# A two-layer decoder trunk on one core: the tile of right-hand operands begins 64 bytes later

## The chip, the cores and the metric

The kernel runs on one core of a Trainium2 chip, as one program in one launch. The metric is the device time in microseconds (us). A core has a matrix engine (TensorE, PE in the profile; PEld is its loading of weights), a vector engine (DVE), a scalar engine (ACT), GpSimd (POOL) and SyncE (SP), which here only issues transfers. They share an on-chip memory (SBUF) of 128 partitions, in which a tile takes the same bytes of every partition.

## The reference

The trunk has 512 tokens of 1024 features and two layers. Everything is float32.

```
h = x
for i in range(DEPTH):
    h = h + 0.5 * swiglu(rms_norm(h, norm_ffn_a[i]), ffn_a_wg[i], ffn_a_wu[i], ffn_a_wd[i])
    hn = rms_norm(h, norm_mix[i])
    mix = even_mixer(hn, ...) if i % 2 == 0 else odd_mixer(hn, ...)
    h = h + mix
    h = h + 0.5 * swiglu(rms_norm(h, norm_ffn_b[i]), ffn_b_wg[i], ffn_b_wu[i], ffn_b_wd[i])
    gate = jax.nn.sigmoid(rms_norm(h, norm_ple[i]) @ ple_gate[i])
    h = h + gate * (p[i] @ ple_proj[i])
return rms_norm(h, final_norm)

def swiglu(h, wg, wu, wd):
    return (jax.nn.silu(h @ wg) * (h @ wu)) @ wd
```

The even mixer runs a sparse attention over the 128 best keys beside a differential attention; the odd one a mixture of three dilated windows. The hidden width of a feed-forward block is 2816.

## The kernel before, in words

The residual stream lies transposed in eight tiles `h0` to `h7`, 128 features by 512 tokens each. Every float32 operand of a large product is split into a high part and a rest, both in the type float32r, and a product is three matmuls: high by high, high by rest, rest by high. In a matmul one operand is stationary (128 columns, loaded as weights ahead of it) and the other moves through, 256 to 512 columns here.

The tile `xr` (line 57) holds right-hand operands: 128 partitions by 2 parts (high, rest) by 7168 float32r. It is allocated once, behind `h7`, and is followed in the code by `hid` (hidden activations, line 63), `hl` (split weights, five slots, line 66) and `fr` (raw weights and scratch, line 69). Tiles of the pool are laid one behind the other in the order of the code; `xr` begins on a multiple of 128 bytes, as do `hid`, `hl` and `fr`. Three things use `xr`:

- In the feed-forward blocks it is seen as `xr[:, part, op, i, :]` (line 58): seven combinations `op` of the halves of the normed input, four blocks `i`, 256 columns each, so 1024 bytes in a row. `right` (line 363) builds them: ACT copies the high part (line 372), DVE takes the rest (line 373). `rest` (line 383) fills two of the seven late. `pair` (line 451) runs a Strassen-like scheme of seven products over them into the accumulators X, Y and Z; its matmul is line 463, with `hl` stationary and `xr` moving. `down` (line 502) multiplies the hidden activations from `hid` with the next weights, by way of `mm3` (lines 306 to 309); it does not touch `xr`. The steps of `pair` and `down` alternate in an order that `plan_ffn` writes out.
- In the mixers the columns from 3072 on of both parts hold the normed input as `xh` and `xl` (lines 59 and 60, written by lines 352 and 353). There it is the stationary operand of `project` (line 608), and `hl` moves. The weight pieces of the first projection hold two rows of 456 columns each, 1824 bytes; those of the others hold rows of 256 or 384 columns.
- The columns ahead of these hold the values of the attention in the mixers (`vts`, line 61, lines 747 and 748), stationary in `attend`; and some operands of the gated embeddings (line 361) and of an output projection (line 755).

Weights are loaded by DMA into `fr`, split by ACT (line 173) and DVE (line 175) into a slot of `hl`, and used from there; a sum of weights that the scheme needs is made by DVE at line 164. A framework orders the instructions of each engine and places the semaphores.

Of the kernel before, what the change touches and what calls it, by code (L numbers as in the profile page):

```python
# [12 lines left out]
F32R = mybir.dt.float32r  # L13
# [5 lines left out]
P = 128  # L19
# [19 lines left out]
def trunk(ctx, tc, a, stop=None):  # L39
# [3 lines left out]
    const = ctx.enter_context(tc.tile_pool(name="const", bufs=1))  # L43
# [10 lines left out]

    hT = [const.tile([P, NT], F32, tag=f"h{c}", name=f"h{c}") for c in range(KD)]

    xrt = const.tile([P, 2, 7168], F32R, tag="xr", name="xr")
    xr = xrt.rearrange("p s (o i n) -> p s o i n", o=7, i=4)
    xh = [xrt[:, 0, 3072 + c * NT : 3072 + (c + 1) * NT] for c in range(KD)]
    xl = [xrt[:, 1, 3072 + c * NT : 3072 + (c + 1) * NT] for c in range(KD)]  # L60
# [1057 lines left out]
```

## Time and profile before

| | us |
|---|---|
| median of 3 runs | 2203.91 |
| lowest, highest | 2203.74, 2205.78 |
| the profiled execution | 2205.18 |
| its span, first to last instruction | 2203.4 |
| PE busy in the span | 2081.2 |
| DVE, ACT, POOL busy | 1698.5, 1068.8, 281.2 |

The profile shows one execution. Busy time counts an instance from its start to its end and overlapping ones once; a matmul's end lies some way behind the start of the next, so what one costs in a stream is read from the distance of the starts in the timeline, not from its duration. The mean granted clock of TensorE is 0.966 of its full 2.4 GHz over the span. In the views below "X<-xr,hl" means that the instruction writes X and reads xr and hl, and 128x256 is partitions by elements.

### The profile page before, as it was taken

To read this page: it belongs to the slowest core of one execution; us is meant where nothing else is said; L and a number is where in the kernel's file an instruction comes from. 1 tells how busy PE (TensorE), PEld (TensorE's weight loads), DVE (VectorE), ACT (ScalarE), POOL (GpSimd) and SP (SyncE) were. 2 spreads that over 40 slices of the span, in tenths; PEclk is the share of its full clock that TensorE was granted. 3 is DMA by queue.
4 is the path that set the end of the run, shared out by engine and by line. 5 is a ranking of instruction groups with operands and counts; after the bars stand their busy time and mean duration, and the time that the engine had idled before them with its cause. 6 is when DMAs were issued, how large, how long until landed. Compare 5 with 4: busy or idle time off the path is not lost.

```text
span 2203.4 us, 34325 instructions
## 1 busy us (share of the span) xinstructions
PE 2081.2 (94%) x13283; PEld 1906.9 (87%) x13283; DVE 1698.5 (77%) x2682; ACT 1068.8 (49%) x1722; POOL 281.2 (13%) x249
## 2 busy tenths in 40 slices
PE   4999999998787899999999999999999879999998
PEld 3999998988676899999789999989989769999986
DVE  7888776688987887786688877767656688877775
ACT  4544444355555454443455444445656545444443
POOL 2000000433411000000320000014324110000011
PEclk6999999999899899999999999999999979999999
DMA  4333233321211233333233333222212214333331
GB/s 128 106 104 100 86 95 104 79 60 47 61 39 39 77 96 106 111 102 94 84 95 101 101 101 115 87 80 77 68 48 71 77 39 121 94 93 107 108 111 41
DMA packets 302051, 190.06 MB, mean 86 GB/s; under 512 B 14208, under 2 KB 292800, under 8 KB 301888
## 3 DMA queue, kind: packets, MB, share of 16 engines
q1 hardware_dynamic: 298592, 184.36, 28.5%
q10 hardware_dynamic: 2912, 2.46, 0.4%
q8 instruction: 104, 1.70, 0.3%
q0 software_dynamic: 384, 1.05, 0.2%
q14 instruction: 59, 0.48, 0.1%
HBM read 185.73 MB, written 2.10 MB: 85 GB/s over the span
## 4 chain that ended last, share of the span: by engine, by line
PE 85%; DVE 11%; issue 1%; ACT 1%; DMA 1%; POOL 0%; SPq 0%; DVEq 0%; POOLq 0%; ACTq 0%
PE X L463 23%; PE Y L463 11%; PE down L308 7%; PE down L307 7%; PE down L309 7%; PE Z L463 6%; PE proj L307 3%; PE proj L308 3%; PE proj L309 3%; DVE fr L164 1%; DVE xr L373 1%; PE outp L308 1%; PE outp L307 1%; PE pt L716 1%; PE outp L309 1%
## 5 line engine op out<-in xcount | busy, mean ns | idle before, releaser
L173 ACT ACTIVATE hl<-fr 128x1024 fp32r<-128x1024 f32 (+5 forms) x620 | 521.8, 860 | 681.8 <-PE X L463 301.7
L175 DVE TENSOR_TENSOR hl<-fr,hl 128x1024 fp32r<-128x1024 f32 (+2 forms) x485 | 548.0, 1137 | 164.7 <-ACT hl L173 159.2
L463 PE MATMUL X<-xr,hl 128*128 128x256 f32 x4224 | 551.4, 286 | 27.8 <-DVE xr L373 25.0
L463 PEld LDWEIGHTS X<-xr,hl 128*128 128x128 f32 x4224 | 534.0, 194 | 39.5 <-DVE xr L373 29.0
L463 PE MATMUL Y<-xr,hl 128*128 128x256 f32 x2112 | 279.6, 287 | 19.9 <-ACT xr L372 11.2
L463 PEld LDWEIGHTS Y<-xr,hl 128*128 128x128 f32 x2112 | 265.2, 194 | 26.7 <-ACT xr L372 12.5
L308 PE MATMUL down<-hid,hl 128*128 128x512 f32 x704 | 274.8, 390 | 0.0
L307 PE MATMUL down<-hid,hl 128*128 128x512 f32 x704 | 274.7, 390 | 0.0
L309 PE MATMUL down<-hid,hl 128*128 128x512 f32 x704 | 274.3, 390 | 0.0
L164 DVE TENSOR_TENSOR fr<-fr 128x1024 f32<-128x1024 f32 x176 | 218.8, 1244 | 23.1 <-DMA fr<-in_ffn_b_wu_dram 11.1
L175 POOL TENSOR_TENSOR hl<-fr,hl 128x512 fp32r<-128x512 f32 (+3 forms) x135 | 155.6, 1170 | 270.2 <-ACT hl L173 220.5
L307 PE MATMUL proj<-hl,xr 128*128 128x384 f32 (+2 forms) x512 | 170.1, 335 | 5.6 <-DVE fr L632 4.3
L308 PE MATMUL proj<-hl,xr 128*128 128x384 f32 (+2 forms) x512 | 170.0, 333 | 0.0
L309 PE MATMUL proj<-hl,xr 128*128 128x384 f32 (+2 forms) x512 | 169.9, 334 | 0.0
L309 PEld LDWEIGHTS down<-hid,hl 128*128 128x128 f32 x704 | 132.3, 188 | 26.8
L307 PEld LDWEIGHTS down<-hid,hl 128*128 128x128 f32 x704 | 132.4, 188 | 26.0
L308 PEld LDWEIGHTS down<-hid,hl 128*128 128x128 f32 x704 | 132.5, 188 | 24.8
L463 PE MATMUL Z<-xr,hl 128*128 128x256 f32 x1056 | 149.6, 284 | 1.1 <-ACT hl L173 0.9
L463 PEld LDWEIGHTS Z<-xr,hl 128*128 128x128 f32 x1056 | 137.1, 193 | 1.7 <-ACT hl L173 1.2
L640 POOL TENSOR_TENSOR fr<-fr 128x512 f32<-128x512 f32 (+1 forms) x72 | 90.9, 1268 | 222.4 <-DVE fr L632 106.6
L512 DVE TENSOR_TENSOR fr<-down,fr 128x512 f32<-128x512 f32 x128 | 87.9, 687 | 22.7 <-PE down L309 21.8
L307 PEld LDWEIGHTS proj<-hl,xr 128*128 128x128 f32 x512 | 98.0, 191 | 7.6 <-DVE fr L632 4.5
(211 smaller groups left out, 2925.5 us busy)
## 6 DMA issues: line engine op xcount, KB each, us to landing
fr<-in_ffn_a_wg_dram SPq DMA_DIRECT2D x88, 256.0 KB, 3.1
fr<-in_ffn_a_wu_dram SPq DMA_DIRECT2D x88, 256.0 KB, 3.5
fr<-in_ffn_b_wg_dram SPq DMA_DIRECT2D x88, 256.0 KB, 3.1
fr<-in_ffn_b_wu_dram SPq DMA_DIRECT2D x88, 256.0 KB, 3.4
fr<-in_ffn_a_wd_dram SPq DMA_DIRECT2D x48, 384.0 KB, 3.8
fr<-in_ffn_b_wd_dram SPq DMA_DIRECT2D x48, 384.0 KB, 3.7
fr<-in_odd_w_in_dram SPq DMA_DIRECT2D x96, 128.0 KB, 2.4
fr<-in_even_w_in_dram SPq DMA_DIRECT2D x56, 128.0 KB, 2.7
```

The costliest lines, as they stand in the source:

```text
L164: nc.vector.tensor_tensor(src, *(sums[x] if isinstance(x, int) else x.ap() for x in (a, b)), op=ALU.add)
L173: nc.scalar.activation(hi[:, s:e], src[:, s:e], AF.Copy)
L175: eng.tensor_tensor(lo[:, s:e], src[:, s:e], hi[:, s:e].bitcast(F32), op=ALU.subtract)
L307: nc.tensor.matmul(ps, lh, rh, start=first, stop=False)
L308: nc.tensor.matmul(ps, lh, rl, start=False, stop=False)
L309: nc.tensor.matmul(ps, ll, rh, start=False, stop=last)
L373: nc.vector.tensor_tensor(lw, s, h.bitcast(F32), op=ALU.subtract)
L463: nc.tensor.matmul(o, w[lw][:, i, us], xr[:, r, op, i, :], start=start and u == 0 and i == 0 and n == 0, stop=i == 3 and n == 2, skip_grou ...
L512: nc.vector.tensor_tensor(t, ps, state["R"], op=ALU.mult)
L640: nc.gpsimd.tensor_tensor(dst, rv, tv, op=ALU.add)
L716: nc.tensor.transpose(ps[:, off : off + P], es[b][:, c * P : (c + 1) * P], ident)
```

## The change

The tile `xr` becomes 14368 float32r long, 32 more than before, and the kernel uses the 14336 from the 16th on, so that everything in it lies 16 elements, 64 bytes, further on in each partition. The view is then shaped as before. All other tiles stay where they were, up to the 32 elements by which the tile is longer. No other line changes.

```
-    xrt = const.tile([P, 2, 7168], F32R, tag="xr", name="xr")
+    xrt = const.tile([P, 14368], F32R, tag="xr", name="xr")[:, 16:14352].rearrange(
+        "p (s n) -> p s n", s=2)
     xr = xrt.rearrange("p s (o i n) -> p s o i n", o=7, i=4)
```

## Rows read from the trace of the kernel before

**Rows 1.** The page's head: busy time of each engine over the whole span

```profile
span 2203.4 us, 34325 instructions
...
PE 2081.2 (94%) x13283; PEld 1906.9 (87%) x13283; DVE 1698.5 (77%) x2682; ACT 1068.8 (49%) x1722; POOL 281.2 (13%) x249
```

**Rows 2.** The chain that ended last: shares by engine, then by line

```profile
PE 85%; DVE 11%; issue 1%; ACT 1%; DMA 1%; POOL 0%; SPq 0%; DVEq 0%; POOLq 0%; ACTq 0%
PE X L463 23%; PE Y L463 11%; PE down L308 7%; PE down L307 7%; PE down L309 7%; PE Z L463 6%; PE proj L307 3%; PE proj L308 3%; PE proj L309 3%; DVE fr L164 1%; DVE xr L373 1%; PE outp L308 1%; PE outp L307 1%; PE pt L716 1%; PE outp L309 1%
```

**Rows 3.** Busy us (x instructions) by stretch; PEclk is the granted clock

```profile
core 0: us, PE busy (x) PEld busy (x) DVE busy (x) ACT busy (x) POOL busy (x), PEclk, DMA share, GB/s
...
400.00:600.00 200.00, 177.34 (x1072) 162.37 (x1070) 170.63 (x503) 97.90 (x239) 86.95 (x78) 0.93 0.21 57
600.00:800.00 200.00, 172.99 (x1035) 150.60 (x1036) 164.95 (x305) 106.24 (x197) 17.65 (x13) 0.90 0.20 57
800.00:1000.00 200.00, 200.00 (x1426) 189.06 (x1425) 157.74 (x164) 89.20 (x103) 0.00 (x0) 1.00 0.35 103
...
1200.00:1400.00 200.00, 200.00 (x1421) 188.88 (x1420) 161.62 (x169) 90.09 (x105) 0.00 (x0) 1.00 0.33 98
...
1800.00:2000.00 200.00, 200.00 (x1482) 191.63 (x1481) 160.65 (x163) 95.12 (x109) 0.00 (x0) 1.00 0.35 102
```

**Rows 4.** PE groups by line and form: count, busy us, mean ns, idle before

```profile
L463 PE MATMUL X<-xr,hl 128*128 128x256 f32 x4224 | 551.4, 286 | 27.8 <-DVE xr L373 25.0 <-ACT xr L372 2.7
L463 PE MATMUL Y<-xr,hl 128*128 128x256 f32 x2112 | 279.6, 287 | 19.9 <-ACT xr L372 11.2 <-DVE xr L373 8.7
...
L463 PE MATMUL Z<-xr,hl 128*128 128x256 f32 x1056 | 149.6, 284 | 1.1 <-ACT hl L173 0.9 <-DVE hl L175 0.2
...
L307 PE MATMUL proj<-hl,xr 128*128 128x384 f32 x384 | 130.6, 342 | 1.3 <-DVE xr L748 1.3
```

**Rows 5.** Timeline of PE, 62 to 80 us: start us, us, line, count

```profile
66.80 5.92 PE L463 MATMUL X<-xr,hl 128*128 128x256 f32 x48
72.56 3.04 PE L463 MATMUL Y<-xr,hl 128*128 128x256 f32 x24
75.44 0.40 PE L463 MATMUL Z<-xr,hl 128*128 128x256 f32 x2
```

**Rows 6.** Timeline of PE in the first projections, 378 to 450 us

```profile
403.73 0.37 PE L307 MATMUL proj<-hl,xr 128*128 128x456 f32 x1
403.94 0.36 PE L308 MATMUL proj<-hl,xr 128*128 128x456 f32 x1
...
412.00 0.37 PE L309 MATMUL proj<-hl,xr 128*128 128x456 f32 x1
412.22 0.28 PE L307 MATMUL proj<-hl,xr 128*128 128x256 f32 x1
412.33 0.28 PE L308 MATMUL proj<-hl,xr 128*128 128x256 f32 x1
412.45 0.28 PE L309 MATMUL proj<-hl,xr 128*128 128x256 f32 x1
...
412.93 0.28 PE L307 MATMUL proj<-hl,xr 128*128 128x256 f32 x1
```

**Rows 7.** Timeline of PE, 1310 to 1322 us: a down step behind line 463

```profile
1314.41 3.04 PE L463 MATMUL X<-xr,hl 128*128 128x256 f32 x24
1317.29 0.40 PE L308 MATMUL down<-hid,hl 128*128 128x512 f32 x1
...
1318.45 0.39 PE L307 MATMUL down<-hid,hl 128*128 128x512 f32 x1
...
1321.85 0.39 PE L307 MATMUL down<-hid,hl 128*128 128x512 f32 x1
```

**Rows 8.** Groups of DVE, then of ACT, by form; columns as in rows 4

```profile
L175 DVE TENSOR_TENSOR hl<-fr,hl 128x1024 fp32r<-128x1024 f32 x324 | 395.2, 1228 | 114.2 <-ACT hl L173 110.7 <-DMA fr<-in_x_dram 2.4 <-PE rbc L340 0.7
...
L373 DVE TENSOR_TENSOR xr<-fr,xr 128x1024 fp32r<-128x1024 f32 x16 | 23.0, 1440 | 6.5 <-ACT xr L372 6.3
...
L373 DVE TENSOR_TENSOR xr<-fr,xr 128x768 fp32r<-128x768 f32 x12 | 13.6, 1129 | 0.0
...
L173 ACT ACTIVATE hl<-fr 128x1024 fp32r<-128x1024 f32 x324 | 339.5, 1058 | 453.6 <-PE X L463 241.4 <-DVE fr L164 73.5 <-PE Y L463 48.0
...
L372 ACT ACTIVATE xr<-fr 128x1024 fp32r<-128x1024 f32 x16 | 16.9, 1054 | 16.9 <-DVE fr L379 16.7
```

**Rows 9.** Waits of PE, longest in total first: us, times, longest us

```profile
PE X L463 <- DVE xr L373: 25.0, 12, 4.5
PE Y L463 <- ACT xr L372: 11.2, 4, 4.6
PE Y L463 <- DVE xr L373: 8.7, 8, 2.1
```

## The prediction

> **What bounds the kernel now.** I read the page's head first: TensorE (PE) is busy for 94% of the span, VectorE (DVE) for 77%, ScalarE (ACT) for 49% [rows 1]. A busy PE can still wait inside, so the chain that ended last comes next: 85% of it is PE, 11% DVE, and line 463, the Strassen-like products of the feed-forward blocks, holds 23 + 11 + 6 = 40% of it [rows 2]. Then the stretches: in 800 to 1000, 1200 to 1400 and 1800 to 2000 us PE has no idle time at all, at a granted clock of 1.00 (its 2.4 GHz level), while DVE is busy for 158 to 162 us of 200. In the mixers (400 to 800 us) PE is idle for 23 to 27 us of 200 and its clock averages 0.90 to 0.93 [rows 3]. So a nanosecond on a matmul of line 463 is a nanosecond on the end; on a matmul of the mixers it is worth a little less.
>
> The change touches only where operands lie. The question is what a matmul costs from start to start, which the busy times and the means do not give: matmuls overlap, and 4224 times 286 ns [rows 4] would be over half the span. Starts do. 48 matmuls of tile X with 256 columns start from 66.80 and the next tile at 72.56: 5.76 us / 48 = 120.0 ns; the next 24 take 2.88 us, 120.0 ns again [rows 5]. At 2.4 GHz 256 columns are 106.7 ns, so 13.3 ns go beside the columns. With 512 columns, where neither operand is in the moved tile, 15 matmuls from 1318.45 to 1321.85 take 226.7 ns each, 213.3 + 13.3 [rows 7]. In a projection xr is the stationary operand: four matmuls of 256 columns from 412.45 to 412.93 take 120 ns each [rows 6]. So the gap is 13.3 ns whether xr streams, is loaded as weights, or is absent. 13.3 ns is 32 columns at this clock.
>
> **The change part by part.** It removes no instruction, adds none, moves none in any queue, and adds no wait; no DMA is issued elsewhere, and none writes or reads xr (the weights land in fr). What it does to each reader and writer of xr:
>
> 1. The moving operand of line 463: 4224 + 2112 + 1056 = 7392 matmuls [rows 4], 7392 x 120.0 ns = 887 us, which fits the 40% of the chain, 881 us [rows 2]. All read 256 elements, 1024 bytes in a row, starting at multiples of 1024 bytes behind the tile's begin; now they start 64 bytes further. No row shows a moving operand at 64 bytes off, so I bound it. The nearest row is the projection with 456 columns: its weight pieces hold two rows of 1824 bytes, so every second moving operand starts 32 bytes off a multiple of 64. 41 of these matmuls from 403.73 to 412.22 take 8.49 us, 207.1 ns each, against 190.0 ns of columns: a gap of 17.1 ns, 3.7 more than elsewhere [rows 6]. If odd starts cost that: 7392 x 3.7 ns = 27 us. But the row tells more. 1824 bytes are 28.5 blocks of 64; paid in whole blocks they are 464 columns, 193.3 + 13.3 = 206.7 ns, and 207.1 was measured. In whole blocks of 32 bytes (57, no remainder) it would be 203.3, in blocks of 128 bytes (15, 480 columns) 213.3. The grain that fits is 64 bytes, and in that grain 1024 bytes starting 64 further are 16 blocks as before: 0. With a grain of 128 they would touch 9 blocks for 8, 32 columns or 13.3 ns more, 7392 x 13.3 = 99 us; that is the far upper end, against which the 207.1 speaks. Downward the gap cannot fall below nothing: 99 us again, and half of it is 49 us. I take 0, by the nearest row's own arithmetic.
>
> The Trainium skill ("SBUF — State Buffer", Specifications) counts SBUF lines of 16 bytes; by it a shift of four whole lines costs nothing and the sum is unchanged, but by it the 456-column row should also show 13.3 ns, and [rows 6] show 17.1, so its grain is not the whole story here.
>
> 2. The stationary operand from xr: 3 x 512 matmuls of the projections (384 x 3 of them with 384 columns [rows 4]), 336 of the attention sums and 96 of the last gate. The gap is the same 13.3 ns with xr as weights [rows 6] as with hl [rows 5]. 0; at 3.7 ns each at most 1968 x 3.7 = 7 us, of which the mixers' idle time [rows 3] takes some. The 144 matmuls of 512 columns with xr as the moving operand (a gate, an output projection) add 0.5 us at that price.
>
> 3. The writers. ACT copies (line 372) take 1054 ns for 128x1024 into xr in strided pieces, and 1058 ns in one run into hl (line 173): the place of the output makes no difference there. DVE takes 1440 ns at line 373 against 1228 ns at line 175 of the same size [rows 8]; that 212 ns is the nearest bound for what the layout of the output can do. 28 such instructions, 6 us up or down, and of PE's waits those for line 373 are the longest, 25.0 + 8.7 us [rows 9]. The shift moves neither their shape nor their steps: 0. Lines 352, 353, 747 and 748 likewise.
>
> 4. The settling. When PE changes from 256 to 512 columns, five matmuls from 1317.29 to 1318.45 take 232 ns each before 226.7 is reached [rows 7], 26 ns in all. So the two streams that PE reads, columns and next weights, do act on each other for a while. There are 64 down steps in the four blocks; were this doubled or gone in each, 64 x 26 ns = 2 us. I take 0 and keep these 2 us, and some 2 us by which runs differ, as the forecast's own width.
>
> Sum: 0, and the profiled execution's 2205.2 us (span 2203.4 and 1.8 around it) stays; the median of the runs is 2203.9, 1.3 below the profiled one. Forecast 2204 us, its own range 2200 to 2208. About 0.2%, 4.4 us, is what a measurement can tell from no change; on line 463 that is 0.6 ns per matmul.
>
> **The rivals.** *Slower: the gap of line 463 opens.* The streams of columns and weights settle to 13.3 ns when both start at the same place in a block [rows 5, 7], and do not settle where starts alternate [rows 6]. With xr 64 bytes off and hl not, they could stay unsettled at 17.1 ns: 7392 x 3.7 = 27 us, 2231. It decides from 0.6 ns per matmul on. Against it: the even grain of 64 bytes. For it: the settling shows that the streams meet somewhere, and every aligned operand here has the same phase, so no row clears another phase.
>
> *Faster: the 13.3 ns are a collision of the two streams in the same half of a 128-byte block, and the shift takes them apart.* A quarter of the gap is 25 us (2179), half is 49 us (2155). For it: the first matmuls of 256 columns, at 412.22 and 412.33, are 110 ns apart [rows 6], so 120 is no floor. DVE's 79% in these stretches [rows 3] leaves room for it. Against it: the gap is 13.3 ns for 256 and 512 columns alike, as a fixed price of changing weights would be. The Trainium skill ("TensorE: Matmul & The Clock Gate", Part 2) gives PE two independent read ports for columns and weights; by that there is no collision to cure and none to make, 2204 in both rivals' place. The five slow matmuls of [rows 7] are not explained by it.
>
> *The change does more than it says.* The tile is 32 elements longer, so tiles declared behind it may be laid 128 bytes later, and another layout could order instructions otherwise. 128 bytes keep the phase in every grain above; a changed order would show as other waits, of the size of [rows 9], some 10 us either way.
>
> **How the numbers follow.** No change 0.53; slower by the opened gap 0.26; faster 0.17; other layout 0.04, half each side. So faster 0.19, same 0.53, slower 0.28. The range goes from 2176 (the smaller of the faster cases and 3 us of writers and settling) to 2234 (the opened gap and the same 3 us). It leaves out the larger gain, part of the larger losses and the 99 us ends, under 0.2 together.
>
> **What would show it.** Right: 24 matmuls of line 463 still start 2.88 us from those that follow, the down steps stay at 226.7 ns, the chain's shares stay. The slower rival: 2.97 us for 24, with down steps unchanged. The faster: 2.72 to 2.80. Writers: line 373 off 1440 ns. Wrong altogether: a clock below 1.00 in the stretches of [rows 3], or waits of PE in them, where there were none.

## The result and the profile after

The kernel with the moved tile takes 2184.61 us (median, 2182.95 to 2188.01) against 2203.82 us for the kernel before (2203.35 to 2205.78): a ratio of 0.9913, with an interval of 0.9896 to 0.9930. That is 19.2 us, 0.9%, faster. The forecast was no change.

The page's head and the chain of the kernel after; these lines answer to [rows 1] and [rows 2]. Line 463 of before is line 464 here. The instructions of each engine come in the same order as before.

```profile
span 2181.2 us, 34325 instructions
...
PE 2059.2 (94%) x13283; PEld 1885.6 (86%) x13283; DVE 1696.4 (78%) x2682; ACT 1068.1 (49%) x1722; POOL 281.1 (13%) x249
...
PE 84%; DVE 12%; issue 1%; ACT 1%; DMA 1%; SPq 0%; POOL 0%; DVEq 0%; ACTq 0%; POOLq 0%
```

The span is 22.2 us shorter and PE's busy time 22.0 us; DVE, ACT and POOL moved by 2.1, 0.7 and 0.1 us, with the same counts everywhere. So nothing was taken off a wait: the matmuls themselves became shorter. The windows, the groups of line 464 with the idle time ahead of them, PE's waits and the two writers answer to [rows 3], [rows 4], [rows 9] and [rows 8], with the columns of those rows:

```profile
800.00:1000.00 200.00, 200.00 (x1433) 188.73 (x1433) 160.44 (x169) 90.64 (x104) 0.00 (x0) 1.00 0.34 101
...
1800.00:2000.00 200.00, 200.00 (x1488) 190.58 (x1487) 167.63 (x172) 96.66 (x111) 0.00 (x0) 1.00 0.36 107
```

```profile
L464 PE MATMUL X<-xr,hl 128*128 128x256 f32 x4224 | 539.5, 284 | 27.4 <-DVE xr L374 24.5 <-ACT xr L373 2.7
...
L464 PE MATMUL Y<-xr,hl 128*128 128x256 f32 x2112 | 274.2, 285 | 19.8 <-ACT xr L373 11.2 <-DVE xr L374 8.6
```

```profile
PE X L464 <- DVE xr L374: 24.5, 11, 4.5
PE Y L464 <- ACT xr L373: 11.2, 4, 4.6
PE Y L464 <- DVE xr L374: 8.6, 8, 2.1
```

```profile
L374 DVE TENSOR_TENSOR xr<-fr,xr 128x1024 fp32r<-128x1024 f32 x16 | 23.0, 1438 | 6.5 <-ACT xr L373 6.3
...
L373 ACT ACTIVATE xr<-fr 128x1024 fp32r<-128x1024 f32 x16 | 16.9, 1053 | 16.9 <-DVE fr L380 16.7
```

PE is still full in the feed-forward stretches, at the same granted clock of 1.00, but gets through more matmuls in them: 1433 for 1426 and 1488 for 1482 in 200 us. The waits are those of before within 0.5 us, the writers are within 2 ns. What changed is the distance of the starts. The timeline of PE at the places of [rows 5] and at a down step as in [rows 7] (start us, us, line, count):

```profile
65.92 5.82 PE L464 MATMUL X<-xr,hl 128*128 128x256 f32 x48
71.57 2.99 PE L464 MATMUL Y<-xr,hl 128*128 128x256 f32 x24
...
1301.47 2.99 PE L464 MATMUL X<-xr,hl 128*128 128x256 f32 x24
1304.30 0.39 PE L309 MATMUL down<-hid,hl 128*128 128x512 f32 x1
...
1305.43 0.39 PE L308 MATMUL down<-hid,hl 128*128 128x512 f32 x1
```

48 matmuls in 71.57 - 65.92 = 5.65 us are 117.7 ns each, for 120.0 before; 24 in 2.83 us are 117.9. The first five down matmuls behind them take 1.13 us, 226 ns each: the five slow ones of [rows 7] are gone. In another stretch of the same execution, at the start of the second feed-forward block and ahead of its first down step, the same line goes faster still:

```profile
742.50 5.60 PE L464 MATMUL X<-xr,hl 128*128 128x256 f32 x48
747.94 2.88 PE L464 MATMUL Y<-xr,hl 128*128 128x256 f32 x24
750.66 0.39 PE L464 MATMUL Z<-xr,hl 128*128 128x256 f32 x2
```

5.44 us / 48 = 113.3 ns, and 2.72 / 24 = 113.3. So line 464 knows two steady paces here, 113.3 and 117.8 ns, and most of it runs at the slower one: the faster one stands only in such openings, above all of the second and the fourth block (about a quarter of their matmuls); the first block opens at 117.8, and behind a down step it is 117.8 everywhere.

Taken over all matmuls that follow the one before without a wait (6860 and 6856 of the 7392 of this line; the mean distance of their starts, from the trace), the change splits up like this:

| matmul | before, ns | after, ns | count x difference, us |
|---|---|---|---|
| line 463/464, 256 columns | 119.91 | 117.23 | 7392 x -2.68 = -19.8 |
| down, 512 columns | 227.75 | 226.94 | 2112 x -0.81 = -1.7 |
| projections, 384 columns | 174.40 | 173.38 | 1152 x -1.02 = -1.2 |
| gates (tile `pg`), 512 columns | 227.63 | 230.22 | 384 x +2.59 = +1.0 |

The sum, -21.7 us, is what the span lost (-22.2), within 0.5 us.

### The profile page after: what moved, and what is told of

The parts are those of the page before. It is cut to its first block, busy times and chain, and to the rows that moved or that the text cites. A ratio compares the mean times of both kernels' runs of the same rounds, so it can differ in the third digit from the quotient of the medians.

```text
span 2181.2 us, 34325 instructions
## 1 busy us (share of the span) xinstructions
PE 2059.2 (94%) x13283; PEld 1885.6 (86%) x13283; DVE 1696.4 (78%) x2682; ACT 1068.1 (49%) x1722; POOL 281.1 (13%) x249
## 4 chain that ended last, share of the span: by engine, by line
PE 84%; DVE 12%; issue 1%; ACT 1%; DMA 1%; SPq 0%; POOL 0%; DVEq 0%; ACTq 0%; POOLq 0%
PE X L464 22%; PE Y L464 11%; PE down L310 7%; PE down L309 7%; PE down L308 7%; PE Z L464 6%; PE proj L308 3%; PE proj L309 3%; PE proj L310 3%; DVE fr L165 1%; DVE xr L374 1%; PE outp L309 1%; PE outp L308 1%; PE outp L310 1%; PE pt L717 1%
## 5 line engine op out<-in xcount | busy, mean ns | idle before, releaser
L464 PE MATMUL X<-xr,hl 128*128 128x256 f32 x4224 | 539.5, 284 | 27.4 <-DVE xr L374 24.5
L464 PEld LDWEIGHTS X<-xr,hl 128*128 128x128 f32 x4224 | 522.4, 191 | 39.4 <-DVE xr L374 28.6
L464 PE MATMUL Y<-xr,hl 128*128 128x256 f32 x2112 | 274.2, 285 | 19.8 <-ACT xr L373 11.2
L464 PEld LDWEIGHTS Y<-xr,hl 128*128 128x128 f32 x2112 | 259.9, 191 | 26.5 <-ACT xr L373 12.5
```

The source lines that it names most:

```text
L464: nc.tensor.matmul(o, w[lw][:, i, us], xr[:, r, op, i, :], start=start and u == 0 and i == 0 and n == 0, stop=i == 3 and n == 2, skip_grou ...
```

## The experiments

What an operand's place can do, in three theories. A: what counts is the distance in bytes between the columns that stream and the weights that are loaded beside them. B: what counts is the place of the streaming columns by itself. C: `xr` does nothing; the later tiles, which the longer tile pushes 128 bytes on, do it. The tiles lie one behind the other; that of `xr` is 57344 bytes long before and that of `hid` 49152, both multiples of 256, so `hl` lies a multiple of 256 behind both. After, the tile of `xr` is 57472 bytes long and its used part begins 64 bytes into it, so `xr` stands 64 bytes short of a multiple of 256 from `hl`, written -64 below, and `hid` at 0. Each table entry below is a mean distance of starts, as above.

**The push alone.** `xr` stays, and the 128 bytes lie behind it.

```
-    xrt = const.tile([P, 2, 7168], F32R, tag="xr", name="xr")
+    xrt = const.tile([P, 14368], F32R, tag="xr", name="xr")[:, 0:14336].rearrange(
...
```

> xr keeps its place and only gets the 32 spare elements behind it, so that hid, hl and fr lie 128 bytes further, as they do in the changed kernel. Theory A (the place of the streamed columns relative to the weights, within 128 bytes, sets the gap of line 463): nothing changes, 2204 us, 120.0 ns per matmul of line 463. Rival C (it was the 128-byte move of the later tiles): 2185 us, about 117 ns.

**Only the weights move.** `hl` 64 bytes further, `xr` and `hid` stay.

```
-    hlt = const.tile([P, NHL, 2, 1024], F32R, tag="hl", name="hl")
+    hlt = const.tile([P, 10272], F32R, tag="hl", name="hl")[:, 16:10256].rearrange(
...
```

> xr and hid stay, hl moves by 64 bytes. Theory A (relative place): line 463 falls to about 117.3 ns as in the changed kernel, 7392 x 2.7 = 20 us gained; but the 2112 down matmuls of 512 columns now also have columns and weights 64 bytes apart, and the few 512-column matmuls with that distance in the changed kernel took about 233 instead of 227 ns, so 2112 x 6 = 13 us are lost: about 2197 us. Rival B (the absolute place of xr): 2204 us, 120.0 ns.

**All three move.** `xr`, `hid` and `hl` each 64 bytes into a tile that is 128 longer.

```
-    hidt = const.tile([P, 24, NT], F32R, tag="hid", name="hid")
+    hidt = const.tile([P, 12320], F32R, tag="hid", name="hid")[:, 16:12304].rearrange(
...
```

(`xr` as in the change, `hl` as in the experiment ahead.)

> xr, hid and hl all move by 64 bytes, so that no distance between columns and weights in the feed-forward blocks changes within 128 bytes. Theory A (relative place): 2204 us, 120.0 ns on line 463. Rival B (the absolute place of xr): 2185 us, about 117 ns.

**The change upside down.** `xr` stays; `hid` and, behind it, `hl` stand 64 bytes further.

```
-    hidt = const.tile([P, 24, NT], F32R, tag="hid", name="hid")
+    hidt = const.tile([P, 12304], F32R, tag="hid", name="hid")[:, 16:12304].rearrange(
...
```

> xr stays, hid and hl both move by 64 bytes: within 128 bytes the distance of columns and weights is that of the changed kernel for line 463 (64) and for down (0), but with the other side moved. Theory A (only the distance counts): as the changed kernel, 2185 us, line 463 at about 117 ns and down at 227. Theory A2 (the distance decides, but which of several rhythms PE settles in also hangs on where the down steps before leave it, as the 113 ns of the run with hl alone moved suggests): line 463 below 120 ns, down anywhere from 227 to 233, 2170 to 2195 us. Rival B (the absolute place of xr): 2204 us, 120 ns.

| kernel | `xr` off `hl`, bytes | `hid` off `hl` | line 464, ns | down, ns | median, us | ratio |
|---|---|---|---|---|---|---|
| before | 0 | 0 | 119.91 | 227.75 | 2203.8 | 1 |
| after | -64 | 0 | 117.23 | 226.94 | 2184.6 | 0.9913 |
| the push alone | -128 | 0 | 119.52 | 228.28 | 2203.1 | 0.9997 [0.9988, 1.0007] |
| only the weights | -64 | -64 | 113.96 | 233.03 | 2177.2 | 0.9877 [0.9862, 0.9891] |
| all three | 0 | -128 | 119.86 | 232.53 | 2214.7 | 1.0050 [1.0036, 1.0065] |
| upside down | -64 | 0 | 116.99 | 226.93 | 2180.8 | 0.9902 [0.9885, 0.9918] |

The timelines of PE, first of the push alone, then of only the weights, of all three, and of the change upside down:

```profile
748.51 5.86 PE L464 MATMUL X<-xr,hl 128*128 128x256 f32 x48
754.21 3.01 PE L464 MATMUL Y<-xr,hl 128*128 128x256 f32 x24
```

```profile
791.25 2.88 PE L464 MATMUL Y<-xr,hl 128*128 128x256 f32 x24
793.97 0.39 PE L464 MATMUL Z<-xr,hl 128*128 128x256 f32 x2
...
804.85 0.39 PE L308 MATMUL down<-hid,hl 128*128 128x512 f32 x1
...
806.94 0.40 PE L308 MATMUL down<-hid,hl 128*128 128x512 f32 x1
```

```profile
749.23 5.92 PE L466 MATMUL X<-xr,hl 128*128 128x256 f32 x48
754.99 3.04 PE L466 MATMUL Y<-xr,hl 128*128 128x256 f32 x24
```

```profile
792.27 2.99 PE L464 MATMUL X<-xr,hl 128*128 128x256 f32 x24
795.10 2.99 PE L464 MATMUL Y<-xr,hl 128*128 128x256 f32 x24
```

5.70 / 48 = 118.8 ns with the push alone, and no gain: C falls. With only the weights moved, `xr` has not moved by a byte and its matmuls take 2.72 / 24 = 113.3 ns; with all three moved, `xr` stands where the change put it in its tile and they are back at 5.76 / 48 = 120.0. The change upside down moves everything but `xr` and has the change's numbers, 2.83 / 24 = 117.9. So B falls. The place of the weights by itself falls too: `hl` lies 64 bytes off its old place, counted in 256, both in "only the weights" (114.0 ns) and in "all three" (119.9). A stands, for both lines: the down matmuls, nine of them from 804.85 to 806.94, take 232 ns as soon as the weights leave `hid` by 64. At 512 columns the same distance costs what it saves at 256: in "only the weights" line 464 gives 7392 x 5.95 = 44.0 us, down takes 2112 x 5.28 = 11.2 back, and gates and output projections another 3 us; all classes of matmuls come to 30.8 us, and the span is 27.9 us shorter. Theory A's expectation of 2197 us was too high by 20: it took 117.3 ns for line 464, which went to 114.0.

In "all three" the down step was expected to be as before, and took 232.5 ns. `hid` and `hl` are then 128 bytes apart, because the tile of `hid` is itself 128 longer. So 128 is not the same as 0, and the pattern had to be mapped.

**The map.** One view of `xr` (and of `hid`, where it says so) for each of the four feed-forward blocks in the order in which they run, each at another offset in one longer tile; all else stays a multiple of 256 apart. So each value comes from one block of one execution, some 1700 distances of starts; in the kernel before, the four blocks lie between 119.89 and 119.92 ns. The offset is counted past a multiple of 256, so that it has the other sign than the 64 of the change.

```
+    XO, HO = (4, 8, 12, 16), (4, 8, 12, 16)
+    xrf = const.tile([P, 14400], F32R, tag="xr", name="xr")
+    xrs = [xrf[:, o : o + 14336].rearrange("p (s o i n) -> p s o i n", s=2, o=7, i=4) for o in XO]
...
+        xr, hidt = xrs[k], hids[k]
```

`xr` and `hid` both by 16, 32, 48, 64 bytes:

> In the four feed-forward blocks, in the order in which they run, xr (256 columns, line 463) and hid (512 columns, down) both begin 16, 32, 48 and 64 bytes later; in the mixers and the gates both stay. Theory A, with a grain of 64 bytes: 16, 32 and 48 bytes cost at least the rounding of one block, so line 463 at 120 ns or more (up to 127) and only the fourth block at 117; with a gap that falls steadily with distance: 119, 119, 118, 117. Down at 64 bytes about 233 ns by the few matmuls of that kind in the changed kernel; between 227 and 233 at the others.

`xr` and `hid` both by 80, 96, 112, 128:

> In the four blocks xr and hid both begin 80, 96, 112 and 128 bytes later. If the gap of line 463 falls with the distance from the last multiple of 128 (9.5, 10.5, 11.7, 8.3 ns were seen at 16, 32, 48, 64, against 13.3 at 0, so it does not fall steadily), no clear forecast: between 113 and 120 ns at 80 to 112, and 120 at 128 if the pattern repeats after 128. Down, which took 231 to 233 ns at 16 to 48 and 229 at 64: 229 to 233 at 80 to 112, 227 at 128.

`xr` alone by 0, 128, 256, 384:

> In the four feed-forward blocks, in the order in which they run, xr alone begins 0, 128, 256 and 384 bytes later. If the pattern of places repeats after 128 bytes, all four blocks have line 463 at 120 ns. If it repeats after 256, blocks 1 and 3 are alike and 2 and 4 are alike; the run with 128 bytes behind xr showed line 463 spread from 115 to 123 instead of a steady 120, so blocks 2 and 4 would look like that, with a mean of 119 to 120.

`xr` alone by 64, 192, 320, 448:

> The same with 64, 192, 320 and 448 bytes. Repeats after 128: all four near one value, 114 to 117 ns. Repeats after 256: 1 and 3 alike, 2 and 4 alike, all below 120 if 64 bytes of distance is what helps. If down alone sets the rhythm, all four at 117 as in the changed kernel, since hid and hl keep their distance.

`xr` alone by 48, 80, 96, 112:

> In the four feed-forward blocks xr alone begins 48, 80, 96 and 112 bytes later; hid and hl keep their distance, so down should be at 227 ns in all. With hid moved too, line 463 took 118.3, 118.4, 120.1 and 114.0 ns there. If the distance in line 463 alone decides, the same four values; if the down steps decide too, others, between 113.3 and 120.

| distance, bytes past a multiple of 256 | 0 | 16 | 32 | 48 | 64 | 80 | 96 | 112 | 128 |
|---|---|---|---|---|---|---|---|---|---|
| line 464, `hid` moved too, ns | | 116.16 | 117.14 | 118.34 | 114.93 | 118.44 | 120.13 | 113.97 | 118.64 |
| down beside it, ns | | 231.5 | 233.3 | 231.7 | 228.9 | 231.1 | 233.2 | 231.0 | 232.7 |
| line 464, `xr` alone, ns | 119.91 | | | 118.38 | 117.81 | 119.89 | 120.00 | 113.79 | 119.53 |

With `xr` alone the down matmuls stay at 226.8 to 228.4 ns in every block. 256 and 384 bytes gave 119.88 and 119.54, the values of 0 and 128; 192, 320 and 448 gave 116.72, 117.47 and 117.34, near the 117.81 of 64, in blocks that mix the two paces differently. So the pattern repeats after 256 bytes. The first map fits neither of its two forecasts: with a grain of 64 bytes, 16, 32 and 48 bytes should have cost 120 ns or more, and took 116 to 118, and the gap does not fall steadily either. With `xr` alone 48, 96 and 112 bytes gave what they gave beside a moved `hid`, but 64 and 80 took 117.8 and 119.9 for 114.9 and 118.4, so what runs between the products counts too. And the expected repeat after 128 is wrong: 0 and 128 differ for 512 columns (227 against 232.7), and at 128 the starts of line 464 scatter around 119.5 where at 0 they stand at 120.0 (at 80 and 96 they scatter around 120). The lowest value of the map is at 112. For 512 columns the sign counts: 228.9 ns at +64, 233.0 at -64 (only the weights). The timeline of PE with `xr` alone moved, in the third block (96 bytes), then in the fourth (112):

```profile
1245.20 3.04 PE L472 MATMUL Y<-xr,hl 128*128 128x256 f32 x24
1248.09 3.04 PE L472 MATMUL X<-xr,hl 128*128 128x256 f32 x24
...
1834.70 2.88 PE L472 MATMUL X<-xr,hl 128*128 128x256 f32 x24
1837.42 1.29 PE L472 MATMUL Z<-xr,hl 128*128 128x256 f32 x10
```

2.89 / 24 = 120.4 ns against 2.72 / 24 = 113.3.

**Two paces at 64 bytes.** The change has 117.8 ns in most products and 113.3 only in openings of blocks; with `hid` also off by 64 (only the weights; 64 in the first map) 113.3 is the commoner. Theory: the pace is inherited from what PE ran just before, so that a product behind down matmuls at distance 0 starts in step with them and stays at 117.8. Two trials, both on top of the change. First: the hidden tiles `f` 4 and 5 stand 64 bytes further, so that products come behind down matmuls at that distance. The first of the four sections of a block has only four hidden tiles, so its down steps stay at 0.

```
...
+        at = f + 4 * low if f < 4 else 8 + (f - 4) + 2 * low
+        return 6208 * half + at * NT + (16 if f > 3 else 0)
...
```

> The changed kernel, with the last two hidden tiles of a section (f = 4 and 5, high and rest) laid 64 bytes further, so that the last 12 matmuls of a down step have columns and weights 64 bytes apart and the others none. Theory A2 (at a distance of 64 bytes line 463 has two rhythms, 113.3 and 117.8 ns, and the down step before decides which): entered from such matmuls, most products run at 113.3 as with hl alone moved, 7392 x 4 = 30 us gained, against 704 matmuls x 6 ns = 4 us lost: 2155 to 2165 us. If the rhythm is decided by the distance in line 463 alone and the 113.3 ns of the run with hl moved came from hl's own place: 2185 + 4 = 2189 us, 117 ns.

It took 2183.44 us, 0.9913 [0.9898, 0.9927]: the change's own time. The timeline, from the first of the last six down matmuls, which are moved ones:

```profile
870.39 0.40 PE L321 MATMUL down<-hid,hl 128*128 128x512 f32 x1
...
871.78 2.99 PE L477 MATMUL X<-xr,hl 128*128 128x256 f32 x24
874.61 2.99 PE L477 MATMUL Y<-xr,hl 128*128 128x256 f32 x24
```

The six moved ones take 1.39 / 6 = 232 ns each, and the product behind them 2.83 / 24 = 117.9, the change's pace; over the kernel down rose to 229.6. Apart from openings of blocks only one product in each block, inside a down step, went at 113.3. The moved ones are 576, not the 704 of the expectation. The pace did not tip, and the theory in this form missed. One rival is left: here `hid` stands at +64 and `xr` at -64, where "only the weights" has -64 for both and the first map +64 for both, so down matmuls at the product's own signed distance weren't tried. Second: the first matmul of a product that doesn't open its accumulator is cut into two of 128 columns, 176 more matmuls, to break the step.

```
-                            nc.tensor.matmul(o, w[lw][:, i, us], xr[:, r, op, i, :],
...
+                            cut = not start and u == 0 and i == 0 and n == 0
+                            for cs in (slice(0, 128), slice(128, 256)) if cut else (slice(0, 256),):
+                                nc.tensor.matmul(o[:, cs], w[lw][:, i, us], xr[:, r, op, i, cs],
...
```

> The changed kernel, with the first matmul of each product that goes on with an accumulator cut into two of 128 columns: 176 matmuls more. If any disturbance ahead of a product can tip line 463 from 117.8 into 113.3 ns: up to 7392 x 4 = 30 us gained, less 176 x some 20 ns = 3.5 us, 2160 to 2180 us. If the rhythm comes back by itself after a disturbance: 2188 us, line 463 at 117 ns.

```profile
879.86 2.99 PE L466 MATMUL Y<-xr,hl 128*128 128x256 f32 x24
882.68 0.40 PE L466 MATMUL Z<-xr,hl 128*128 128x256 f32 x2
882.92 3.02 PE L466 MATMUL X<-xr,hl 128*128 128x128 f32 x25
885.78 3.01 PE L466 MATMUL Y<-xr,hl 128*128 128x128 f32 x25
```

A cut product (25 matmuls) takes 885.78 - 882.92 = 2.86 us, an uncut one 2.82. Behind a cut the starts soon stand 113.3 ns apart, until the next down step, so the pace did tip, but the two halves and the matmul behind them take 59 + 111 + 173 = 343 ns in the mean where two whole ones took 236: 107 ns x 176 = 19 us, all that the better pace gave. The expectation had some 20 ns for a cut. 2188.33 us, 0.9936 [0.9919, 0.9952], no better than the change. So the pace depends on what was run just before; which earlier instruction selects it isn't settled.

**The version that the map points to.** `xr` 112 bytes off, in a tile that is 256 longer so that `hid` and `hl` keep their distance.

```
-    xrt = const.tile([P, 14368], F32R, tag="xr", name="xr")[:, 16:14352].rearrange(
+    xrt = const.tile([P, 14400], F32R, tag="xr", name="xr")[:, 28:14364].rearrange(
...
```

> The kernel before with xr 112 bytes further and 256 bytes longer, so that hid, hl and fr keep their places modulo 256. The map with xr alone at 112 bytes had line 463 at 113.8 ns and down at 227.8 in its block. If that holds in all four blocks: 7392 x 6.2 ns = 46 us below 2203, 2157 us, below the changed kernel by 27 us. If the block was a lucky entry into the 113.3 ns rhythm: between 2157 and 2185 us. The projections, whose weights come from xr, may go up or down by some 2 us.

2162.4 us (2160.5 to 2163.2), 0.9812 [0.9799, 0.9826]: 40 us under the kernel before and 22 under the change, the fastest of all. Its page's head, its group of line 464 and its timeline just behind a down step:

```profile
span 2161.0 us, 34325 instructions
...
PE 2038.3 (94%) x13283; PEld 1862.2 (86%) x13283; DVE 1695.4 (78%) x2682; ACT 1068.9 (49%) x1722; POOL 280.7 (13%) x249
```

```profile
L464 PE MATMUL X<-xr,hl 128*128 128x256 f32 x4224 | 525.4, 279 | 27.5 <-DVE xr L374 24.7 <-ACT xr L373 2.7
```

```profile
807.23 0.39 PE L310 MATMUL down<-hid,hl 128*128 128x512 f32 x1
807.45 2.92 PE L464 MATMUL X<-xr,hl 128*128 128x256 f32 x24
810.21 2.88 PE L464 MATMUL Y<-xr,hl 128*128 128x256 f32 x24
812.93 0.39 PE L464 MATMUL Z<-xr,hl 128*128 128x256 f32 x2
```

The first 24 take 2.76 us, the next 2.72: at 112 bytes line 464 finds 113.3 ns by itself behind a down step, where in the change it stays at 117.8. Over the kernel it takes 113.81 ns, 7392 x 6.10 = 45 us less; the projections with 384 columns (+0.9 ns) and the gates (+3.0) give 2 us back. All classes of matmuls together come to 42.1 us, and the span is 42.4 us shorter. Of the 5 us by which it lies above the expected 2157, the projections, the gates and the output projections (0.3) account for 2.4; the rest isn't traced.

## Why the prediction was wrong

*The bound.* Right. PE is full in the stretches named, and a nanosecond on line 464 was a nanosecond on the end: 19.8 us out of 2.68 ns, in a span that fell by 22.2.

*Step 1, the moving operand.* This step failed. It took 0 for what the shift does to the gap of 13.3 ns, and the gap fell to 10.5, 2.7 ns on each of 7392 matmuls. Two arguments stood behind the 0. The first was the arithmetic of the 456-column row [rows 6], whose 17.1 ns I read as whole blocks of 64 bytes, so that a shift by one whole block should be free. The map refutes the reading: a whole block, 64 bytes, gives 117.8 ns, and 80 and 96 bytes, which are none, give 120 in the mean as 0 does. Nor did the 456-column matmuls answer to the shift: 207 ns in the mean before, after and at 112 bytes, within half a nanosecond. A row in which start, length and distance vary at once was made to say which of them counts. The second was that the gap is 13.3 ns whether `xr` streams, is weights, or is absent, as a fixed price of changing weights would be. All those rows had one thing in common that I noted and gave too little weight: every aligned operand stood at distance 0 from its partner. Agreement among them could not tell a fixed price from the price of that one distance, and at least half of it was the latter: at 112 bytes 113.3 - 106.7 = 6.7 ns are left. Whether these are a fixed price no run shows.

*The rival "faster".* It named what the runs bear out, that the place of the columns against the weights makes part of the gap, and a size: a quarter of the gap, 25 us, or half, 49. Measured were 2.7 of 13.3 ns, a fifth, and 19.8 us. The 2.72 to 2.80 us for 24 that were to show it stand only in the openings of blocks; elsewhere it is 2.83. Its place, "the same half of a 128-byte block", is wrong: the pattern repeats after 256 bytes, and neither 64 nor 128 takes the streams apart best. What spoke against it, one gap for 256 and 512 columns, holds at distance 0 only; at -64 the gaps are 6.7 or 11.1 ns for 256 columns and 19.7 for 512 (233.0 - 213.3). What spoke for it, the 110 ns between two starts and the five slow down matmuls, deserved more than 0.17.

The Trainium skill ("TensorE: Matmul & The Clock Gate", Part 2) says that loading the next weights takes no read bandwidth from the running matmul, by two independent read ports. In the runs the place of the one still counts for the other: moving the weights alone by 64 bytes changed line 464 from 119.9 to 114.0 ns and down from 227.8 to 233.0. The Trainium skill ("SBUF — State Buffer", Specifications) counts lines of 16 bytes; the map was taken in steps of one such line and goes from 113.8 to 120.1 ns, so whole lines aren't alike.

*The rival "slower".* In the mean the gap of line 464 opened at no distance of the map (120.1 ns at most, for 120.0 at 0). What can open is the gap of the down step: "all three" is slower by 11 us, of which 2112 x 4.8 ns = 10 are down matmuls at a distance of 128.

*Step 2, the stationary operand.* 0 was taken, with 7 us as its bound; the 384-column projections gained 1.2 us and the gates lost 1.0.

*Step 3, the writers.* Right: 1438 ns for 1440, 1053 for 1054.

*Step 4, the settling.* It went away altogether, 226.9 for 227.8 ns in the mean: 1.7 us of the 2 that were kept for it. I read these rows as a sign that the streams meet and then priced them as an end effect only.

*The rival "does more than it says".* The later tiles do lie 128 bytes later, and the order of the instructions is that of before. The push by itself is worth nothing (0.9997); beside the 64 bytes it turns the distance from +64 to -64, and the map has about the same for both (117.8 and, at 192, 116.7). But 128 bytes don't keep the phase, as the prediction has it: down took 232.5 ns with `hid` 128 bytes off (all three), for 227.8.

The time is inside the range because the small form of the faster rival had set its lower end; the forecast's own sum, with its width of 2200 to 2208, missed it.

What stays open: whether the two streams meet, and in which part of the memory or of its paths, why 112 is the best of the places tried and what lies between the steps of 16 bytes or in the upper half of the 256 beside 192, and what selects between the two paces. The runs show the dependence on the distance, not its cause.

## What to carry to other kernels

When TensorE is full, treat the distance in bytes between the streamed operand and the weights, counted in 256, as a size to be tried: it costs some padding, and here it was worth 0.9% at 64 and 1.9% at 112, but tune it for the shape that holds most of the time, since here 512 columns want 0 where 256 want 112. Put several distances into one kernel, one for each repeated block, and read them off the distance of the starts in one timeline. And a price that is the same in all rows is only a fixed price if the rows differ in what you are about to change.

## What the runs showed of the hardware

- The start-to-start time of a float32r matmul depends on the distance between its columns and the weights, and repeats after 256 bytes (0 and 256 alike, 128 and 384 alike): for 256 columns 120.0 ns at 0, 113.8 at 112, about 117 at 64 and 192 beside down matmuls at 0, 120 in the mean at 80 and 96, 119.5 at 128.
- For 512 columns it goes the other way: 227 ns at 0, 229 to 233 at 16 to 128 and 233 at -64.
- At 64 bytes there are two steady paces, 113.3 and 117.8 ns, in one execution; at 0 nearly all starts (98%) stand within 1 ns of 120, and at 112 some 90% at 113 to 114.
- Two halves of 128 columns in place of one matmul of 256 cost 107 ns more with the matmul behind them than two whole ones at 117.8 ns.
